# Sums of squares taken from transposed tiles, and stick-breaking products with v in groups of four key blocks

## The chip, the cores and the metric

One NeuronCore of one Trainium2 chip runs the whole program. The metric is device time in microseconds of one execution; the kernel before was timed in three runs. One further execution was recorded by the hardware profiler, and all stretches and durations below are of that one.

## The reference, cut to what matters

One layer (x is 1024 tokens by 1024 channels, fp32). A normalised x is multiplied by one wide matrix; its columns feed two token mixers and two merge gates.

```
h = RMSNorm(x);  proj = h @ w_in
A (8 heads of 64): z = q k^T / 8, causal; a = sigmoid(z) * prod over later keys of (1 - sigmoid(z)); o = a v
B (4 heads of 128): q, k, v = SiLU(conv4(.)); q, k each divided by sqrt(sum of squares over the 128 channels);
   chunked gated delta rule with k k^T, q k^T, a triangular solve and a scan over chunks; per-head RMSNorm
merged = sigmoid(gA) * (oA @ w_branch_sb) + sigmoid(gB) * (oB @ w_branch_gdn)
out = x + RMSNorm(merged @ w_out)
```

The change touches three places: the sums of squares of q and k in B, the product a v in A, and where some buffers of B and of the last stage are taken from.

## The kernel before, in words

Dense products run on TensorE (PE) as three fp32r matmuls of 512 columns per 128-row piece (high and low parts of both operands, `dense`, L222; `y`, L969). The transposes and the products `kk`, `kq`, `ss` and `av` have fp32 operands. PE takes its instructions in order. The program is written as generators, and `weave` interleaves dense work (`d_...` tiles) with the work that depends on other engines. A scheduler then fixes one order for each engine from the written order, priorities (`load_w` runs ahead) and the time at which it believes a buffer to be free.

Buffers: a slot pool `sp` with 23 slots of 4 KB a partition, a `small` pool in which tag `aT` has 4 buffers of 2 KB, and PSUM in two pools: 3 banks for dense outputs (`psd`) and 5 for all else (`psg`, `gps`). A bank is reused when its last reader is done.

Stages in order, with their time in the profile: the normalised input and first dense products; `g_mid(0)` (some 66 to 125 us), the solve and scan of heads 0 and 1, `g_mid(1)` (some 240 to 295 us), the scan of heads 2 and 3; the attention with its dense side work (500 to 817 us); `ya`, the product of A with its branch matrix (817 to 863 us); the last product `y` in two halves of 8 token tiles (to 953 us).

In `g_mid(b)` the convolved k and q of a head lie with channels on the partitions (`acc_k`, `acc_q`, 128x1024). `sumsq` squares such a tile on ScalarE (ACT, L375), sums over the partitions with eight matmuls against a column of ones (tile `ss_...`, L378) and copies 128x8 sums with VectorE (DVE, L379). `tokens` transposes k, eight 128x128 blocks into two banks (`t_k`, L386), and DVE copies them to `kn` (L387). The sums of k go into `br2`, which multiplies the products `kk` out of PSUM (L426), and those of q into `rqs`.

In the attention (`attention`, L781 onwards) a step is a pair of heads p and a query group g of two 128-query blocks. `sb_z` makes z on PE, two sigmoids on ACT (`kp` L800, `bt` L801), a scan on DVE (L803) and a product on GpSimd (POOL, L804). One step later `sb_av` transposes `bt` key block by key block (`aT`, L820, four 128x128 transposes, two for the last block), copies each out of PSUM (DVE L825 and L827, ACT L829), and multiplies with v (`av`, L834) after every two key blocks. At its end `sgT` is multiplied with `av` (L851).

In the last stage, `y` of a token tile is finished by: ACT squares and sums (L973, `yj` with tag `aT`), DVE multiplies with the norm weight (L978), a short chain for the root (L155 to L161), DVE adds the residual `xr` (L987, twice), and SyncE (SP) issues the output (L988) and the loads of `xr` (L982).

Of the kernel before, what the change touches and what calls it, by code (L numbers as in the profile page):

```python
# [7 lines left out]
F32 = mybir.dt.float32  # L8
# [12 lines left out]
CAP = 60.0  # L21
NSLOT = 23
AB = 4
RUN = 1.9
# [3 lines left out]
def tile_stickbreak_gdn_hybrid(  # L28
# [37 lines left out]
    def slot(name, dt=F32, shape=None):  # L66
        return sp.tile(shape or [P, T], dt, tag="s", name=name)

    def gps(name, shape=None):
        return psg.tile(shape or [P, 512], F32, tag="g", name=name)  # L70
# [301 lines left out]

    def sumsq(src, dst, h, name):
        sq = slot(f"sq_{name}")
        nc.scalar.activation(sq, src, AF.Square)  # L375
        ps = gps(f"ss_{name}")
        for c in range(NT):
            nc.tensor.matmul(ps[:, c:c + 1], lhsT=sq[:, c * P:(c + 1) * P], rhs=ones[:, 0:1], start=True, stop=True)  # L378
        nc.vector.tensor_copy(dst[:, h * NT:(h + 1) * NT], ps[:, :NT])  # L379

    def tokens(src, dst, name):
        for g in range(2):
            ps = gps(f"t_{name}_{g}")
            for j in range(4):
                c = g * 4 + j
                nc.tensor.transpose(ps[:, j * P:(j + 1) * P], src[:, c * P:(c + 1) * P], ident)  # L386
            nc.vector.tensor_copy(dst[:, g * 4:g * 4 + 4], ps.rearrange("p (c j) -> p c j", j=P))  # L387

# [106 lines left out]
    def g_lev(hs, last):  # L495
        lx, lxt = lane_out[hs[0] // 2]
        Xb, Xt = {}, {}
        for h in hs:
# [5 lines left out]
            for r in range(4):  # L504
# [3 lines left out]
                nc.sync.dma_start(Xb[h][rs, :, o:o + 32], lx[h % 2, r].rearrange("c i j -> i c j"))  # L508
        V1 = small.tile([P, 2, NT, 32], F32, tag="aT", name=f"V1_{hs[0]}", bufs=AB)
        ps = gps(f"V1p_{hs[0]}")  # L510
# [38 lines left out]
        for h in hs:  # L549
            V2[h] = small.tile([64, NT, 64], F32, tag="aT", name=f"V2_{h}", bufs=AB)  # L550
            src = pv[h][:64].rearrange("p (c j) -> p c j", j=64)
            if h % 2:
                nc.vector.tensor_scalar(V2[h], src, -1.0, None, op0=ALU.mult)
            else:
                nc.scalar.mul(V2[h], src, -1.0)
# [123 lines left out]
    def g_mid(b, prev):  # L679
        h0, h1 = 2 * b, 2 * b + 1  # L680
        bs = slice(b * 16, b * 16 + 16)
        drain(g_q(h0))
        for h in (h0, h1):
            kn[h] = slot(f"kn_{h}", shape=[P, NT, P])
            sumsq(kT[h], ssk, h, f"k{h}")
            tokens(kT[h], kn[h], f"k{h}")
        li = g_m(b)
        drain(g_q(h1))
        for h in prev:
            g_o(h)  # L690
        sumsq(qT[h0], ssq, h0, f"q{h0}")
        g_i(h0)
        drain(g_v(h0))
        drain(g_v(h1))
        sumsq(qT[h1], ssq, h1, f"q{h1}")
        rsqrt(rqs[:, bs], ssq[:, bs], 1.0, 16)
        nc.vector.tensor_scalar(rqs[:, bs], rqs[:, bs], float(P) ** -0.5, None, op0=ALU.mult)
        g_i(h1)
        last = lanes(b, li)
        ahead[0] = 600  # L700
        drain(fill(1))
        g_vt(h0)
        drain(fill(1))
        g_vt(h1)
        drain(fill(2), g_gate(h0), g_gate(h1))
        ahead[0] = 200
        return chain(g_lev((h0, h1), last), g_scan((h0, h1)))
# [72 lines left out]

    def sb_z(p, g):  # L781
        K, vn, gT, Q = sbd[p]
        QH, QL = Q[g // 2]
        for a in range(2):
            for j in range(2):
# [21 lines left out]
    def sb_av(p, g):  # L807
# [4 lines left out]

        def tr(c):
            j0 = 1 if c == cl else 0
            ps = gps(f"aT_{p}_{g}_{c}")
            for a in range(2):
                for j in range(j0, 2):
                    qb = 2 * g + j
                    off = c * P - (T - (qb + 1) * P)
                    nc.tensor.transpose(ps[:, (a * 2 + j) * P:(a * 2 + j + 1) * P], at[p, a, qb][:, off:off + P], ident)  # L820
            aT = small.tile([P, 4, P], F32, tag="aT", name="aT", bufs=AB)
            dst = aT.rearrange("p (a j) q -> p a j q", a=2)[:, :, j0:]
# [9 lines left out]
        def mm(c, j0, aT):  # L832
            for a in range(2):
                nc.tensor.matmul(av[a * 64:(a + 1) * 64, j0 * P:2 * P], lhsT=vn[:, c, a * 64:(a + 1) * 64],  # L834
                                 rhs=aT[:, a * 2 + j0:a * 2 + 2], start=(c == NT - 1), stop=(c == cl))

        q = []
        for c in range(NT - 1, cl - 1, -2):
            n = []
            for e in (c, c - 1):  # L840
                n.append(tr(e))
                yield 0.43
            for e in q:
                mm(*e)
            if q:
                yield 0.9
            q = n
        for e in q:
            mm(*e)
        yield 0.9  # L850
        nc.vector.tensor_tensor(gT[:, gq], gT[:, gq], av[:, :2 * P], op=ALU.mult)  # L851

    def attention():
        pend = []
        for p in range(NP):
            for g in range(NT // 2):
                yield from sb_z(p, g)
                pend.append((p, g))
                if len(pend) > 1:
                    yield from sb_av(*pend.pop(0))  # L860
            yield None
        yield from sb_av(*pend.pop(0))

# [90 lines left out]
    for n in range(2):  # L954
        ns = slice(n * HT, (n + 1) * HT)
        for t in range(NT):
# [8 lines left out]
            for c0, c1 in zip(cuts, cuts[1:]):  # L965
                ps = psd.tile([P, c1 - c0], F32, tag="d", name=f"y_{t}_{n}_{c0}")
                for k in range(NK):
                    for i, (a, b) in enumerate(((m_hi, wo[n, k][0]), (m_hi, wo[n, k][1]), (m_lo, wo[n, k][0]))):
                        nc.tensor.matmul(ps, lhsT=a[:, k, ts_], rhs=b[:, c0:c1], start=(k == 0 and i == 0),  # L969
                                         stop=(k == NK - 1 and i == 2))  # L970
                junk = small.tile([P, 4, P], F32, tag="aT", name="yj", bufs=AB)
                ss = small.tile([P, 1], F32, tag="ssy", name="ssy")
# [44 lines left out]
```

## Time and profile before

| what | before |
|---|---|
| median of 3 runs | 961.71 us (961.5 to 962.51) |
| the profiled execution | 960.5 us, of which the span of its instructions is 958.8 |
| busy share of the span | PE 98%, DVE 62%, ACT 39%, POOL 19% |
| granted TensorE clock | 0.999 of 2.4 GHz over the span |

Times in rows count from the start of the span. A row `start us, us, engine line op out<-in xcount` is one instruction or a run of equal ones. PE's matmuls are pipelined, and their ends are modelled: a row of a 128x512 product shows 0.39 us, and the next starts 0.227 us later. What a run of matmuls costs is read from its start to the start of the next row. Matmuls of fp32 operands stand as two records each.

### The profile page before, as it was taken

Reading aid. Unit: us, or ns where it says so; the run is one execution under the profiler, and the core shown is the slowest. Engines: PE = TensorE matmul, PEld = TensorE weight load, DVE = VectorE, ACT = ScalarE, POOL = GpSimd, SP = SyncE. Lnnn points to the kernel's source line nnn. Section 1 sums busy time; section 2 is a strip of 40 time slices with the busy share of each in tenths; the row PEclk is TensorE's granted clock in tenths of the full one; section 3 lists DMA queues with packets and bytes.
Section 4 is the critical chain, followed back from the end, with each engine's and each line's share of the span. In section 5 each row is a group of like instructions: output and inputs, shape, how many; then the busy total and the mean of one; then the engine's idle time right before and its main releaser. Section 6 shows DMA issues by size and latency. Waiting matters only on the chain.

```text
span 958.8 us, 13556 instructions
## 1 busy us (share of the span) xinstructions
PE 939.3 (98%) x5290; PEld 770.5 (80%) x5290; DVE 594.4 (62%) x1074; ACT 375.8 (39%) x741; POOL 185.1 (19%) x113
## 2 busy tenths in 40 slices
PE   8999999999999999999999999999999999999997
PEld 7978888788888887887877777877887777777886
DVE  5667796356899933656466734693675575573244
ACT  6664432135455112543244333462443453232221
POOL 1011210001113000000044212360533363341000
PEclk9999999999999999999999999999999999999999
DMA  7013324300221341005721121020011202772152
GB/s 254 14 45 95 98 72 132 67 24 23 67 77 56 110 115 40 12 23 184 235 77 45 29 60 44 23 67 23 23 44 44 78 34 64 248 266 80 58 193 102
DMA packets 88419, 80.12 MB, mean 84 GB/s; under 512 B 17098, under 2 KB 74531, under 8 KB 88355
## 3 DMA queue, kind: packets, MB, share of 16 engines
q1 hardware_dynamic: 86944, 79.20, 26.6%
q8 instruction: 41, 0.67, 0.3%
q10 hardware_dynamic: 1410, 0.07, 0.1%
q14 instruction: 24, 0.19, 0.1%
HBM read 60.88 MB, written 18.37 MB: 83 GB/s over the span
## 4 chain that ended last, share of the span: by engine, by line
PE 84%; DVE 7%; issue 3%; ACT 3%; DMA 2%; POOL 1%; DVEq 0%; ACTq 0%; POOLq 0%
PE d_mg L222 13%; PE y L969 8%; PE d_q L222 5%; PE d_sv L222 5%; PE d_gg L222 5%; PE d_v L222 5%; PE d_sk L222 5%; PE d_yb L222 4%; PE d_sq L222 4%; PE d_sgt L222 4%; PE av L834 4%; PE d_ya L222 3%; DVE kp L803 3%; PE aT L820 3%; PE d_k L222 2%
## 5 line engine op out<-in xcount | busy, mean ns | idle before, releaser
L804 POOL TENSOR_TENSOR bt<-bt,kp 128x127 f32<-128x127 f32 (+3 forms) x64 | 123.0, 1940 | 370.2 <-DVE kp L803 307.4
L803 DVE TENSOR_TENSOR_SCAN kp<-kp,mscan 128x128 f32<-128x128 f32 (+3 forms) x64 | 106.5, 1694 | 24.3 <-ACT kp L800 24.1
L222 PE MATMUL d_mg<-h_hi,whi_mg 128*128 128x512 f32 x256 | 101.5, 397 | 0.1
L222 PE MATMUL d_mg<-h_lo,whi_mg 128*128 128x512 f32 x256 | 100.1, 391 | 0.0
L222 PE MATMUL d_mg<-h_hi,wlo_mg 128*128 128x512 f32 x256 | 100.0, 391 | 0.0
L800 ACT ACTIVATE kp<-z 128x384 f32<-128x384 f32 (+4 forms) x96 | 49.6, 517 | 67.1 <-PE z L798 55.7
L222 PEld LDWEIGHTS d_mg<-h_hi,whi_mg 128*128 128x128 f32 x256 | 48.1, 188 | 10.9 <-issue 1.1
L222 PEld LDWEIGHTS d_mg<-h_hi,wlo_mg 128*128 128x128 f32 x256 | 48.1, 188 | 10.0
L222 PEld LDWEIGHTS d_mg<-h_lo,whi_mg 128*128 128x128 f32 x256 | 48.2, 188 | 9.3
L801 ACT ACTIVATE bt<-z 128x384 f32<-128x384 f32 (+4 forms) x96 | 50.1, 522 | 8.3 <-DMA mB_d<-mb 5.8
L969 PE MATMUL y<-wohi,m_lo 128*128 128x512 f32 (+1 forms) x136 | 51.4, 378 | 0.9 <-DVE m_lo L926 0.9
L969 PE MATMUL y<-wohi,m_hi 128*128 128x512 f32 (+1 forms) x136 | 51.4, 378 | 0.3 <-ACT m_hi L925 0.3
L969 PE MATMUL y<-wolo,m_hi 128*128 128x512 f32 (+1 forms) x136 | 51.3, 377 | 0.0
L834 PE MATMUL av<-aT,svn 128*64 128x256 f32 (+1 forms) x320 | 39.0, 369 | 3.5 <-DVE aT L825 1.2
L370 POOL TENSOR_TENSOR acc_k<-acc_k,pre_k 128x1024 f32<-128x1024 f32 x4 | 9.6, 2388 | 165.3 <-ACT pre_k L369 165.3
L820 PE MATMUL aT<-ident,bt 128*128 128x128 f32 x288 | 38.5, 276 | 2.2 <-DVE svn L772 1.8
L820 PEld LDWEIGHTS aT<-ident,bt 128*128 128x128 f32 x288 | 32.4, 140 | 9.8 <-issue 4.6
L834 PEld LDWEIGHTS av<-aT,svn 128*64 128x64 f32 x320 | 20.2, 136 | 20.5 <-issue 9.7
L89 ACT CAST whi_mg<-raw_mg 128x1024 fp32r<-128x1024 f32 x16 | 16.8, 1052 | 47.7 <-PE d_mg L222 25.5
L973 ACT ACTIVATE yj<-y 128x512 f32<-128x512 f32 (+1 forms) x17 | 9.7, 573 | 63.7 <-PE y L969 61.2
L941 POOL TENSOR_TENSOR sA<-sA,mBl 128x512 f32<-128x512 f32 x16 | 24.1, 1517 | 48.0 <-DVE sA L940 48.0
L90 DVE TENSOR_TENSOR wlo_mg<-raw_mg,whi_mg 128x1024 fp32r<-128x1024 f32 x16 | 23.3, 1454 | 13.6 <-ACT whi_mg L89 8.5
(381 smaller groups left out, 2448.0 us busy)
## 6 DMA issues: line engine op xcount, KB each, us to landing
raw_mg<-in_w_in_dram SPq DMA_DIRECT2D x16, 512.0 KB, 4.1
mg_d<-mg SPq DMA_DIRECT2D x16, 512.0 KB, 3.0
x<-in_x_dram SPq DMA_DIRECT2D x8, 512.0 KB, 6.9
mb<-mg_d SPq DMA_DIRECT2D x8, 512.0 KB, 5.8
mB_d<-mb SPq DMA_DIRECT2D x8, 512.0 KB, 3.7
sA<-mg_d SPq DMA_DIRECT2D x8, 512.0 KB, 6.8
mBl<-mB_d SPq DMA_DIRECT2D x8, 512.0 KB, 5.4
rawo<-in_w_out_dram SPq DMA_DIRECT2D x8, 512.0 KB, 4.9
```

The costliest lines, as they stand in the source:

```text
L89: nc.scalar.copy(hi[:, :nk], raw[:, :nk])
L90: nc.vector.tensor_sub(lo[:, :nk], raw[:, :nk], hi[:, :nk].bitcast(F32))
L222: nc.tensor.matmul(ps, lhsT=a[:, k], rhs=b[:, hs], start=(k == 0 and i == 0), stop=(k == nk - 1 and i == 2))
L800: nc.scalar.activation(kp[:, os_], ps[:, :pc], AF.Sigmoid, scale=-0.125)
L801: nc.scalar.activation(bt[:, os_], ps[:, :pc], AF.Sigmoid, scale=0.125)
L803: nc.vector.tensor_tensor_scan(kp[:, :n], kp[:, :n], mscan[:, :n], 1.0, op0=ALU.mult, op1=ALU.max)
L804: nc.gpsimd.tensor_tensor(bt[:, 1:n], bt[:, 1:n], kp[:, 0:n - 1], op=ALU.mult)
L820: nc.tensor.transpose(ps[:, (a * 2 + j) * P:(a * 2 + j + 1) * P], at[p, a, qb][:, off:off + P], ident)
L834: nc.tensor.matmul(av[a * 64:(a + 1) * 64, j0 * P:2 * P], lhsT=vn[:, c, a * 64:(a + 1) * 64], rhs=aT[:, a * 2 + j0:a * 2 + 2], start=(c == ...
L941: nc.gpsimd.tensor_tensor(ga[:, hs], ga[:, hs], mb[:, hs], op=ALU.add)
L969: nc.tensor.matmul(ps, lhsT=a[:, k, ts_], rhs=b[:, c0:c1], start=(k == 0 and i == 0), stop=(k == NK - 1 and i == 2))
L973: nc.scalar.activation(junk.rearrange("p a b -> p (a b)")[:, :c1 - c0], ps, AF.Square, accum_out=ss)
```

## The change

Two helpers, `sumsq` and `tokens`, become one. For k and for q it makes the eight transposes first; ACT then squares each transposed 128x128 block straight out of PSUM and adds along the row (`accum_out`, L384 of the new file), and only for k are the banks copied to `kn`. The matmuls with ones and the copies of their sums are gone. In the attention `sb_z` is called for each half (one head of the pair), `sb_av` multiplies after four key blocks, and its last run with the product on `gT` is handed back (`finish`, `late`) and placed between the halves of a later `sb_z`. `V1`, `V2`, `aT` (in pairs) and `yj` take slots of the slot pool, which has 25 now; tag `aT` is gone.

```diff
-NSLOT = 23
-AB = 4
+NSLOT = 25
...
-    def sumsq(src, dst, h, name):
-        sq = slot(f"sq_{name}")
-        nc.scalar.activation(sq, src, AF.Square)
-        ps = gps(f"ss_{name}")
-        for c in range(NT):
-            nc.tensor.matmul(ps[:, c:c + 1], lhsT=sq[:, c * P:(c + 1) * P], rhs=ones[:, 0:1], start=True, stop=True)
-        nc.vector.tensor_copy(dst[:, h * NT:(h + 1) * NT], ps[:, :NT])
-
-    def tokens(src, dst, name):
+    def sumsq(src, dst, h, name, keep=None):
+        pg = []
         for g in range(2):
             ps = gps(f"t_{name}_{g}")
             for j in range(4):
                 c = g * 4 + j
                 nc.tensor.transpose(ps[:, j * P:(j + 1) * P], src[:, c * P:(c + 1) * P], ident)
-            nc.vector.tensor_copy(dst[:, g * 4:g * 4 + 4], ps.rearrange("p (c j) -> p c j", j=P))
+            pg.append(ps)
+        for g, ps in enumerate(pg):
+            for j in range(4):
+                c = g * 4 + j
+                junk = small.tile([P, P], F32, tag="jk", name="jk")
+                nc.scalar.activation(junk, ps[:, j * P:(j + 1) * P], AF.Square,
+                                     accum_out=dst[:, h * NT + c:h * NT + c + 1])
+            if keep is not None:
+                nc.vector.tensor_copy(keep[:, g * 4:g * 4 + 4], ps.rearrange("p (c j) -> p c j", j=P))
...
+        def finish(q):
+            for e in q:
+                mm(*e)
+            yield 0.45 * len(q)
+            nc.vector.tensor_tensor(gT[:, gq], gT[:, gq], av[:, :2 * P], op=ALU.mult)
+
         q = []
-        for c in range(NT - 1, cl - 1, -2):
+        for c in range(NT - 1, cl - 1, -4):
             n = []
-            for e in (c, c - 1):
-                n.append(tr(e))
-                yield 0.43
+            for e in range(c, max(c - 4, cl - 1), -2):
+                pair = slot(f"aT_{p}_{g}_{e}", shape=[P, 2, 4, P])
+                for i in range(2):
+                    n.append(tr(e - i, pair[:, i]))
+                    yield 0.43
             for e in q:
                 mm(*e)
...
+        return finish(q)
...
-                yield from sb_z(p, g)
+                yield from sb_z(p, g, 0)
+                yield from late
+                late = iter(())
+                yield from sb_z(p, g, 1)
                 pend.append((p, g))
                 if len(pend) > 1:
-                    yield from sb_av(*pend.pop(0))
+                    late = yield from sb_av(*pend.pop(0))
...
-                junk = small.tile([P, 4, P], F32, tag="aT", name="yj", bufs=AB)
+                junk = slot(f"yj_{t}_{n}_{c0}", shape=[P, 4, P])
```

The order that the scheduler makes of it moves at three places. The first is PE in `g_mid(0)`, where `t_` are transposes, `ss_` the matmuls with ones, `kk` the products of k with itself and `d_q1` dense work. Before:

```order
L222 MATMUL d_q1_0_966<-h_hi_189,wlo_q1_962 128x512
L378 MATMUL ss_k0_823<-ones_136,sq_k0_821 128x1 x8
L386 MATMUL t_k0_0_833<-ident_111,acc_k0_740 128x128 x4
L386 MATMUL t_k0_1_839<-ident_111,acc_k0_740 128x128 x4
L222 MATMUL d_q1_0_966<-h_hi_189,whi_q1_961 128x512
...
L378 MATMUL ss_k1_848<-ones_136,sq_k1_846 128x1 x8
L386 MATMUL t_k1_0_858<-ident_111,acc_k1_747 128x128 x4
L386 MATMUL t_k1_1_864<-ident_111,acc_k1_747 128x128 x4
L421 MATMUL kk_0_0_885<-acc_k0_740 128x128 x4
```

and now:

```order
L390 MATMUL rw_730<-ident_111,GG_715 32x128
L378 MATMUL t_k0_0_821<-ident_111,acc_k0_740 128x128 x4
L378 MATMUL t_k0_1_826<-ident_111,acc_k0_740 128x128 x4
L378 MATMUL t_k1_0_850<-ident_111,acc_k1_747 128x128 x4
L378 MATMUL t_k1_1_855<-ident_111,acc_k1_747 128x128 x4
L421 MATMUL kk_0_0_893<-acc_k0_740 128x128 x4
...
L378 MATMUL t_q0_0_1033<-ident_111,acc_q0_813 128x128 x4
L221 MATMUL d_v0_0_1089<-h_hi_189,whi_v0_1084 128x512
L221 MATMUL d_v0_0_1089<-h_lo_190,whi_v0_1084 128x512
L378 MATMUL t_q0_1_1038<-ident_111,acc_q0_813 128x128 x4
```

Both heads' transposes of k now stand in one row ahead of the first `kk`; twelve dense matmuls lie between `kk_0_0` and the other three `kk`, and the transposes of q0 stand behind all four.

The second place is PE in the attention of the first pair of heads, third query group. Before:

```order
L820 MATMUL aT_0_2_4_4932<-ident_111,bt_0_1_5_4640 128x128
L834 MATMUL av_0_2_4874<-aT_4880,svn_0_4000 64x256 x2
L834 MATMUL av_0_2_4874<-aT_4887,svn_0_4000 64x256 x2
L820 MATMUL aT_0_2_3_4943<-ident_111,bt_0_0_4_4598 128x128
...
L834 MATMUL av_0_2_4874<-aT_4894,svn_0_4000 64x256 x2
L834 MATMUL av_0_2_4874<-aT_4937,svn_0_4000 64x256 x2
L834 MATMUL av_0_2_4874<-aT_4948,svn_0_4000 64x256 x2
L834 MATMUL av_0_2_4874<-aT_4953,svn_0_4000 64x128 x2
```

and now, where `z_1_..` belongs to the next pair of heads:

```order
L819 MATMUL aT_0_2_2_5004<-ident_111,bt_0_1_5_4741 128x128
L832 MATMUL av_0_2_4943<-aT_0_2_7_4944,svn_0_4072 64x256 x4
L832 MATMUL av_0_2_4943<-aT_0_2_5_4984,svn_0_4072 64x256 x4
L221 MATMUL d_sq1_0_4974<-h_hi_189,whi_sq1_4970 128x512
...
L797 MATMUL z_1_0_1_0_5147<-KA_1_4581,QL_1_0_5032 128x256
L832 MATMUL av_0_2_4943<-aT_0_2_3_4997,svn_0_4072 64x256 x2
L832 MATMUL av_0_2_4943<-aT_0_2_3_4997,svn_0_4072 64x128 x2
L796 MATMUL z_1_1_0_0_5161<-KB_1_4582,QH_1_0_5031 128x128
```

The runs of `av` are fewer and longer, and the last of a group stands between two `z`.

The third place is SP in the last stage (`xr` the residual's loads, `out` the output's stores). Before:

```order
L982 DMA xr_0_7914<-in_x_dram 128x1024
L982 DMA xr_1_7958<-in_x_dram 128x1024
L982 DMA xr_2_8002<-in_x_dram 128x1024
L982 DMA xr_3_8046<-in_x_dram 128x1024
L982 DMA xr_4_8090<-in_x_dram 128x1024
L982 DMA xr_5_8134<-in_x_dram 128x1024
L988 DMA out_0_dram<-y_0_7611 128x512 x2
L982 DMA xr_6_8178<-in_x_dram 128x1024
```

and now:

```order
L990 DMA xr_0_7946<-in_x_dram 128x1024
L996 DMA out_0_dram<-y_0_7643 128x512 x2
L990 DMA xr_1_7990<-in_x_dram 128x1024
L996 DMA out_0_dram<-y_1_7675 128x512 x2
L990 DMA xr_2_8034<-in_x_dram 128x1024
L996 DMA out_0_dram<-y_2_7713 128x512 x2
L990 DMA xr_3_8078<-in_x_dram 128x1024
```

Each load but the first stands behind the two stores of the tile before it, to the end of the program.

## Rows read from the trace of the kernel before

**Rows 1.** The page: busy time and share of each engine; granted clock.

```profile
PE 939.3 (98%) x5290; PEld 770.5 (80%) x5290; DVE 594.4 (62%) x1074; ACT 375.8 (39%) x741; POOL 185.1 (19%) x113
PEclk9999999999999999999999999999999999999999
```

**Rows 2.** Waits of PE, attention's five: releaser: us in total, times, longest.

```profile
PE aT L820 <- DVE svn L772: 1.8, 1, 1.8
PE av L834 <- DVE aT L825: 1.2, 2, 0.6
PE av L834 <- DVE aT L827: 1.1, 1, 1.1
PE av L834 <- ACT aT L829: 1.0, 2, 0.6
PE aT L820 <- ACT bt L801: 0.4, 1, 0.4
```

**Rows 3.** Timeline of PE, 69 to 85 us: `ss`, transposes and `kk`.

```profile
69.66 1.84 PE L378 MATMUL ss_k<-ones,sq_k 128*128 128x1 f32 x16
71.36 1.07 PE L386 MATMUL t_k<-ident,acc_k 128*128 128x128 f32 x8
72.19 0.48 PE L222 MATMUL d_q<-h_hi,whi_q 128*128 128x512 f32 x1
...
80.37 1.07 PE L386 MATMUL t_k<-ident,acc_k 128*128 128x128 f32 x8
81.28 3.74 PE L421 MATMUL kk<-acc_k 128*128 128x128 f32 x32
```

**Rows 4.** PE's groups by shape: two records a matmul with ones, 8 runs.

```profile
L378 PE MATMUL ss_q<-ones,sq_q 128*128 128x1 f32 x64 | 7.6, 248 | 0.2 <-ACT sq_q L375 0.2
L378 PE MATMUL ss_k<-ones,sq_k 128*128 128x1 f32 x64 | 7.4, 245 | 0.0
```

**Rows 5.** ACT, timeline 414 to 415 us: squares of 128x128 with a sum.

```profile
414.12 0.39 ACT L640 ACTIVATE jk<-vb,rqs 128x128 f32<-128x128 f32 x1
414.42 0.19 ACT L640 ACTIVATION_READ_ACCUMULATOR jk<-vb,rqs 128x1 f32 x1
414.51 0.39 ACT L640 ACTIVATE jk<-vb,rqs 128x128 f32<-128x128 f32 x1
```

**Rows 6.** DVE, timeline 81 to 93 us: copies of k, decay tiles, first products on `kk`.

```profile
81.12 1.22 DVE L387 COPY kn<-t_k 128x512 f32<-128x512 f32 x2
...
84.60 2.18 DVE L402 SCALAR_TENSOR_TENSOR D-1.0_0_874<-D-1.0_0_874,GG,capm 128x128 f32<-128x128 f32 x8
86.70 2.19 DVE L402 SCALAR_TENSOR_TENSOR D-1.0_1_907<-D-1.0_1_907,GG,capm 128x128 f32<-128x128 f32 x8
...
89.31 1.12 DVE L426 SCALAR_TENSOR_TENSOR D-1.0_0_874<-kk,br,D-1.0_0_874 128x128 f32<-128x128 f32 x4
```

**Rows 7.** Busy time by stretch: PE, PEld, DVE, ACT, POOL, clock, DMA share, GB/s.

```profile
66.00:95.00 29.00, 28.89 (x171) 25.10 (x170) 22.00 (x71) 14.36 (x18) 2.71 (x2) 1.00 0.26 75
236.00:290.00 54.00, 54.00 (x307) 46.59 (x306) 47.31 (x112) 25.92 (x47) 7.19 (x3) 1.00 0.23 64
```

**Rows 8.** Timeline of PE in the attention: runs of 8 and of 16 records.

```profile
657.51 0.39 PE L222 MATMUL d_sk<-h_hi,wlo_sk 128*128 128x512 f32 x1
657.83 1.08 PE L834 MATMUL av<-aT,svn 128*64 128x256 f32 x8
658.85 0.87 PE L820 MATMUL aT<-ident,bt 128*128 128x128 f32 x6
659.65 1.08 PE L834 MATMUL av<-aT,svn 128*64 128x256 f32 x8
660.66 0.50 PE L222 MATMUL d_sk<-h_hi,whi_sk 128*128 128x512 f32 x1
661.00 0.39 PE L222 MATMUL d_sk<-h_lo,whi_sk 128*128 128x512 f32 x1
...
697.80 1.73 PE L834 MATMUL av<-aT,svn 128*64 128x256 f32 x16
699.47 0.47 PE L797 MATMUL z<-KA,QH 128*128 128x448 f32 x1
```

**Rows 9.** DVE in the last stage: adding the residual, tiles 0, 1 and 7.

```profile
917.27 1.42 DVE L987 SCALAR_TENSOR_TENSOR y<-y,ry,xr 128x512 f32<-128x512 f32 x2
...
921.82 1.41 DVE L987 SCALAR_TENSOR_TENSOR y<-y,ry,xr 128x512 f32<-128x512 f32 x2
...
954.34 1.41 DVE L987 SCALAR_TENSOR_TENSOR y<-y,ry,xr 128x512 f32<-128x512 f32 x2
```

**Rows 10.** SP's queue from 918 us.

```profile
918.05 1.01 SPq L988 DMA_DIRECT2D out_dram<-y  x2
919.11 2.25 SPq L982 DMA_DIRECT2D xr<-in_x_dram  x2
```

**Rows 11.** Issue to landing: the load at 919.11; one at 921; all eight (last line).

```profile
xr<-in_x_dram SPq DMA_DIRECT2D x1, 512.0 KB, 3.8
...
xr<-in_x_dram SPq DMA_DIRECT2D x1, 512.0 KB, 5.1
...
DMA to landing us min/median/max: 3.6/4.8/7.2
```

## What the change should do to the time

> **What bounds the kernel.** I read the page first. PE is busy for 98% of the span at full clock, and no other engine passes 62% [rows 1]. PE takes its instructions in order, so the time is the length of PE's queue, and a gain is either a record less on PE or a wait less in front of one. The waits of PE come next. Of the attention's, those of `av` for a copy just before it make 1.2 + 1.1 + 1.0 = 3.3 us, and two others make 1.8 and 0.4 [rows 2], 5.5 in all. Matmul ends are modelled, so I took each price from the start of a run to the start of the next. Last I read the end of the program, where PE is done and a chain of DVE, SP and a load decides [rows 9 to 11].
>
> **Part 1, the matmuls with ones.** A run of eight (16 records) lasts from 69.66 to 71.36, 1.70 us [rows 3]; there are 128 records, so eight runs [rows 4]. Removed: 8 x 1.70 = 13.6. Added: transposes of q for four heads. Eight transposes take 0.83 (71.36 to 72.19) or 0.91 (80.37 to 81.28) [rows 3]: 4 x 0.87 = 3.5. PE's queue is shorter by **10.1 us**. The transposes of k stay.
>
> The squares move from eight of 128x1024 to 64 of 128x128 on ACT, each with its sum. Such a pair of instructions exists and follows itself every 0.39 us (414.12 to 414.51) [rows 5]: 3.1 us a head. ACT has the time in the mean, 14.4 of 29 us busy in the first of the two stages and 25.9 of 54 in the second [rows 7]; if that cover goes, the price is a wait for a PSUM bank. And some of that wait I expect, since the transposed banks of k are now read by four squares and only then copied by DVE.
>
> In `g_mid(0)` both heads' squares take 16 x 0.39 = 6.2 us and can start when PE has the transposes, about where `ss_k` started, 69.7. So they end near 75.9. In the kernel before DVE needs from its copy of `kn` at 81.12 to the end of the first products on `kk` (89.31 + 1.12 = 90.4), 9.3 us, decay tiles included [rows 6]. The same 9.3 us behind 75.9 give 85.2 for the first bank of `kk`. PE did `kk` from 81.28 for about 3.5 us (3.74 less the modelled end) [rows 3], to 84.8; without two `ss_k` that is 81.4. Eight dense matmuls (1.8), `t_q0_0` (0.45) and two dense ones (0.45) follow, so PE comes at 84.1 to `t_q0_1`, which takes the bank of the first `kk`. It waits 1.0 to 1.4 us; I take 1.3. `kq_0_1` then needs a bank that four squares (1.6 us) still read, of which dense work covers about half: 0.7. Together **+2.0**, between 0 (DVE reaches `kk` sooner) and 5.1 (all that this stage gains, 2 x 1.70 for k and 2 x 0.83 for q).
>
> In `g_mid(1)` DVE is busy 47.3 of 54 us [rows 7]. PE comes earlier by its own gain, DVE doesn't, and the outputs of the earlier heads need banks that DVE frees after its products on `kk`. I put the wait at **+2.0**, between 0 and 5.1 for the same reason. Part 1 sums to -10.1 + 2.0 + 2.0 = -6.1.
>
> The Trainium skill (ScalarE: Activation LUTs, What ACT_TABLE_LOAD costs) gives 186 ns plus 0.833 ns an element for such an ACTIVATE and 93 ns of overlap, so by an estimate from that page 0.20 us a square. No row here shows that, since the square with its sum repeats at 0.39; by the page the squares would end 3 us sooner, both waits of `g_mid(0)` would be gone, and the sum would be 2.0 us lower.
>
> **Part 2, runs of `av`.** Going into a run from a dense matmul costs 0.32 instead of 0.227 (657.51 to 657.83), and the first dense matmul after one 0.34 (660.66 to 661.00). Two runs of 8 records take 1.02 and 1.01 us, one of 16 takes 1.67 (697.80 to 699.47) [rows 8]. So two runs joined save 2.03 - 1.67 = 0.36 and with both edges 0.36 + 0.09 + 0.11 = 0.56; where transposes follow, nearly nothing. I count 33 runs before and 23 after, 10 less, and take the middle, 0.32: **-3.2**, between 0 and -5.6. There are 10 more runs of `z`, for which I see no edge between `z` and dense rows, and put 0.
>
> **Part 3, waits in the attention.** `av` now follows its copies by two more key blocks or, in the late run, by a whole `z`. So the 3.3 us should go. The 1.8 us, a bank that DVE frees behind scans (`svn`), and the 0.4 us for `bt` don't hang on `av`; moved by a little, I let 0.7 of 2.2 go. **-4.0**, between 0 and -5.5 [rows 2]. Four key blocks need four banks of five for their transposes while `av` holds the fifth; I count nothing for it, since the blocks before are copied by then. If that fails, each wait is of the 0.6 us size in rows 2. The pairs of `aT` hold slots that `kp` and `bt` also use; two more slots replace what tag `aT` had, and ACT, which would wait, is 39% busy [rows 1]. At the end of the attention the last multiplications can't be covered by a `z`: **+0.3**, half of such a wait.
>
> **Part 4, the end.** `yj` in slots changes when slots for `xr` come free, and SP now loads `xr` of a tile only behind the stores of the tile before it. DVE's addition (L987) of tile 0 starts at 917.27; the stores go at 918.05, the next load at 919.11, 1.84 us behind the addition [rows 9, 10]. That load took 3.8 us behind two stores, just the new situation [rows 11]. With 0.1 us from landing to start, an estimate, the period is 1.84 + 3.8 + 0.1 = 5.74 us. The additions were 954.34 - 917.27 = 37.1 us apart over seven tiles, 5.30 each [rows 9]. New: 7 x 5.74 = 40.2, so **+3.1**. Bounds: 0 at a landing under 3.36, +1.7 at the shortest seen, 3.6, and +12.2 at the 5.1 of the load at 921 [rows 11]. I take 3.8 because it is the one row with the same neighbours.
>
> The Trainium skill (DMA: Bandwidth & Descriptors, Anatomy of one DMA) has about 2.0 us plus bytes at 436 GB/s, an estimate of 3.2 us for 512 KB. By it the period would be 5.1, PE would set the pace and the sum would be 3.1 us lower; all eight loads here took 3.6 or more, which speaks against it.
>
> **Sum.** -6.1 - 3.2 - 4.0 + 0.3 + 3.1 = -9.9. The profiled execution took 960.5, so 950.6 for one like it. The median of the three runs is 961.71, 1.2 above it: **951.8 us**.
>
> **Rivals.**
> All covered: no new bank waits, all 5.5 us of waits gone, loads no later than PE. -10.1 - 3.2 - 5.5 = -18.8, so 942.9. For it: ACT half idle. Against: DVE in the second stage, and 3.6 as the shortest load. 0.14.
>
> Part 1 given back: DVE, not PE, sets both stages, and PE waits at banks for all that it saved (0 for part 1). -3.2 - 4.0 + 0.3 + 3.1 = -3.8, so 957.9. For it: 47.3 of 54 us of DVE. Against: it still loses eight small copies, and the first stage has 7 of 29 us free. 0.16.
>
> The change to `av` does nothing: the waits come back at other banks, and joined runs are those where transposes follow. -6.1 + 0.3 + 3.1 = -2.7, so 959.0. 0.07.
>
> Slower, by the end's chain alone: loads wait behind stores and land late. The rest is worth -13.0, so it decides at (37.1 + 13.0) / 7 = 7.16 us a tile, a landing of 5.2. At 5.1 it is -0.8, no change; at the longest landing seen, 7.2, the period is 9.14, the end 64.0 - 37.1 = 26.9 later, and the time 975.6. For it: half of the eight loads took 4.8 or more. Against: those were issued several at a time, and here one stands alone. 0.06 for slower, 0.04 for no change.
>
> **How the numbers follow.** The forecast has 0.53. Measurements of this kernel tell some 0.2%, 1.9 us, from no change. The forecast, full cover and the two partial cases are faster, 0.90, less some 0.03 for partial cases that end within 1.9 us: 0.87. Within it 0.04 + 0.02, slower 0.06 + 0.01. The range leaves out half of the full cover at its lower end, and the chain and a little of the partial cases at its upper: 943.5 to 959.5.
>
> **What would show it.** In the new trace: no rows with ones, 64 squares of 0.39 us; PE waiting 1 to 2 us for DVE near 84 us and once in the second stage; some 23 runs of `av`, none waiting on `aT`; L987 about 5.7 us apart, waiting for a load, not for ACT. Wrong if PE waits at banks for more than 5 us in the two stages, if `kp` starts to wait for slots and PE for `kp`'s banks, or if the additions are 5.3 or over 6 us apart.

## The result, and the profile after

| what | before | after |
|---|---|---|
| median of four runs each | 962.11 us (961.5 to 965.39) | 952.41 us (951.52 to 953.58) |
| ratio | | 0.990 [0.988, 0.9921] |
| the profiled execution, its span | 960.5, 958.8 | 953.58, 951.8 |
| granted TensorE clock | 0.999 | 0.996 |

The total came out as forecast (951.8), but not by the forecast's terms. The profiled execution of the new kernel is the slowest of its four, that of the kernel before lies below all its four runs; so the two spans differ by 7.0 us where the medians differ by 9.7. The table splits those 7.0 us at the first and last matmuls of the stages, as the trace has them. The last two columns belong to experiments that are told below.

| stretch, us | before | after | difference | e6_both | e9_later |
|---|---|---|---|---|---|
| start to the first product on `vn` (with `g_mid(0)`) | 126.95 | 122.53 | -4.4 | 122.5 | 121.3 |
| to the first `d_sk` (with `g_mid(1)`) | 234.2 | 232.2 | -2.0 | 234.0 | 232.0 |
| to the first `aT` | 127.5 | 127.2 | -0.3 | 127.3 | 127.2 |
| attention, to the first `d_ya` | 329.5 | 319.7 | -9.8 | 319.7 | 319.7 |
| `ya`, to the first `y` | 45.0 | 49.8 | **+4.8** | 43.8 | 43.8 |
| `y`, to its last matmul | 89.05 | 88.35 | -0.7 | 87.2 | 87.2 |
| last matmul to the end | 6.6 | 12.0 | **+5.4** | 6.6 | 6.6 |

So the parts that were meant to gain gained 16.5 us, and 10.2 us were lost in two stages behind them. First the page of the new kernel, to be held against [rows 1]: PE has 96 records less and is a little less busy, 97% of a shorter span.

```profile
PE 924.6 (97%) x5194; PEld 760.5 (80%) x5194; DVE 591.0 (62%) x1066; ACT 384.9 (40%) x861; POOL 166.4 (17%) x113
PEclk9999999999999999999999999999999999999998
```

The waits of PE in the new kernel (releaser, us in total, times, longest):

```profile
PE d_ya L221 <- DVE wlo_wbs L89: 3.8, 2, 1.9
PE oT L656 <- DVE gg L657: 1.8, 1, 1.8
PE t_q L378 <- DVE D-1.0_0_882 L426: 1.2, 1, 1.2
...
PE d_ya L221 <- DVE sA L948: 1.1, 1, 1.1
PE av L832 <- DVE aT L825: 1.1, 1, 1.1
PE d_mg L221 <- ACT mg L676: 1.0, 1, 1.0
...
PE y L977 <- ACT m_hi L933: 0.5, 1, 0.5
```

Of the attention's five waits [rows 2] one is left, 1.1 us. New are `t_q` in `g_mid(0)`, `oT` and, just behind, `d_mg` in `g_mid(1)`, and 4.9 us for `d_ya`, which waited 0.8 before.

**The squares.** In ACT's timeline they follow one another every 0.25 us, not every 0.39 as those that I took the price from [rows 5]:

```profile
70.36 0.29 ACT L384 ACTIVATE jk<-t_k 128x128 f32<-128x128 f32 x1
70.52 0.23 ACT L384 ACTIVATION_READ_ACCUMULATOR jk<-t_k 128x1 f32 x1
70.61 0.30 ACT L384 ACTIVATE jk<-t_k 128x128 f32<-128x128 f32 x1
```

Sixteen of them are through between 69.23 and 73.6. DVE is not ready for `kk` then. It copies the four banks of `kn` up to 75.1, and one instruction of 128x16 (L149), which takes 0.17 us at 79.10, takes 2.26 us at 76.18. It ends at 78.44, just behind an addition of POOL that ends at 78.41:

```profile
76.18 2.26 DVE L149 TENSOR_SCALAR rst<-rst 128x16 f32<-128x16 f32 x1
```

```profile
76.03 2.38 POOL L369 TENSOR_TENSOR acc_q<-acc_q,pre_q 128x1024 f32<-128x1024 f32 x1 [9.86 <-ACT pre_q L368]
```

DVE reads the first bank of `kk` only from 84.11, and PE's `t_q` starts in that bank 1.18 us later:

```profile
84.11 2.15 DVE L426 SCALAR_TENSOR_TENSOR D-1.0_0_882<-kk,br,D-1.0_0_882 128x128 f32<-128x128 f32 x8
```

```profile
85.29 0.66 PE L378 MATMUL t_q<-ident,acc_q 128*128 128x128 f32 x4 [1.17 <-DVE D-1.0_0_882 L426]
```

**`ya`.** The diff has no line here, but the scheduler orders the whole program, and DVE now does the split of one half (`m_lo`) ahead of the multiplication `sA` of the next. DVE, POOL and ACT of the new kernel, in that stage:

```profile
824.35 0.69 DVE L934 TENSOR_TENSOR m_lo<-sA,m_hi 128x512 fp32r<-128x512 f32 x1 [1.84 <-ACT m_hi L933]
824.96 0.68 DVE L948 TENSOR_TENSOR sA<-sA,d_ya 128x512 f32<-128x512 f32 x1
825.77 1.29 POOL L949 TENSOR_TENSOR sA<-sA,mBl 128x512 f32<-128x512 f32 x1 [2.11 <-DVE sA L948]
827.10 0.62 ACT L933 CAST m_hi<-sA 128x512 fp32r<-128x512 f32 x1 [2.78 <-POOL sA L949]
827.75 0.69 DVE L934 TENSOR_TENSOR m_lo<-sA,m_hi 128x512 fp32r<-128x512 f32 x1 [2.11 <-ACT m_hi L933]
828.36 0.68 DVE L948 TENSOR_TENSOR sA<-sA,d_ya 128x512 f32<-128x512 f32 x1
```

Read down: `sA` at 824.96 releases POOL, POOL releases ACT, ACT releases `m_lo` at 827.75, and only behind that stands the next `sA`, at 828.36. It is a loop over four instructions in which each waits for the one before, 828.36 - 824.96 = 3.4 us a half. A half in which DVE also splits new weights took longer, 832.59 - 828.36 = 4.2. PE needs 12 matmuls of 0.227 us, 2.72 us, for a half. Late as DVE is, its split of the next weights (`wlo_wbs`) comes late too, and PE waits 1.9 us twice for that (the last section shows these two splits). In the kernel before two `sA` stand together, and the loop is cut:

```profile
831.15 0.68 DVE L940 TENSOR_TENSOR sA<-sA,d_ya 128x512 f32<-128x512 f32 x1
832.08 0.69 DVE L940 TENSOR_TENSOR sA<-sA,d_ya 128x512 f32<-128x512 f32 x1 [0.25 <-PE d_ya L222]
```

**The end.** DVE's additions (L995 now) of tiles 0, 1, 5 and 7; then SP's queue; then issue to landing of the eight loads:

```profile
904.86 1.42 DVE L995 SCALAR_TENSOR_TENSOR y<-y,ry,xr 128x512 f32<-128x512 f32 x2
910.95 1.42 DVE L995 SCALAR_TENSOR_TENSOR y<-y,ry,xr 128x512 f32<-128x512 f32 x2 [1.57 <-DMA xr<-in_x_dram]
...
935.01 1.42 DVE L995 SCALAR_TENSOR_TENSOR y<-y,ry,xr 128x512 f32<-128x512 f32 x2 [3.88 <-DMA xr<-in_x_dram]
...
947.42 1.42 DVE L995 SCALAR_TENSOR_TENSOR y<-y,ry,xr 128x512 f32<-128x512 f32 x2 [3.07 <-DMA xr<-in_x_dram]
```

```profile
905.64 1.01 SPq L996 DMA_DIRECT2D out_dram<-y  x2
906.74 0.40 SPq L990 DMA_DIRECT2D xr<-in_x_dram  x1
```

```profile
DMA to landing us min/median/max: 3.5/3.9/4.8
```

From the second on, every addition waits for its load, and the load goes out behind the addition before it: 1.82 to 1.91 us behind in six periods, 3.05 in the one in which SP's two stores (at 935.79) took 2.18 us instead of about 1.0. The additions are (947.42 - 904.86) / 7 = 6.08 us apart, against 5.30 before [rows 9].

### The profile page after: what moved, and what is told of

Same layout as the page of the kernel before. It is cut to its first block, busy times and chain, and to the rows that moved or that the text cites. A ratio compares the mean times of both kernels' runs of the same rounds, so it can differ in the third digit from the quotient of the medians.

```text
span 951.8 us, 13464 instructions
## 1 busy us (share of the span) xinstructions
PE 924.6 (97%) x5194; PEld 760.5 (80%) x5194; DVE 591.0 (62%) x1066; ACT 384.9 (40%) x861; POOL 166.4 (17%) x113
## 4 chain that ended last, share of the span: by engine, by line
PE 81%; DVE 9%; DMA 4%; ACT 2%; issue 2%; POOL 2%; SPq 0%; DVEq 0%; POOLq 0%; ACTq 0%
PE d_mg L221 17%; PE y L977 6%; PE d_sk L221 5%; PE d_sv L221 5%; PE d_gg L221 5%; PE d_sgt L221 5%; PE d_yb L221 4%; PE d_sq L221 4%; PE d_v L221 4%; PE av L832 4%; PE aT L819 3%; PE d_k L221 2%; PE d_k L211 2%; DMA xr<-in_x_dram 2%; PE z L796 2%
## 5 line engine op out<-in xcount | busy, mean ns | idle before, releaser
L803 POOL TENSOR_TENSOR bt<-bt,kp 128x127 f32<-128x127 f32 (+3 forms) x64 | 102.6, 1613 | 380.6 <-DMA mb<-mg_d 155.4
L802 DVE TENSOR_TENSOR_SCAN kp<-kp,mscan 128x128 f32<-128x128 f32 (+3 forms) x64 | 103.8, 1640 | 26.3 <-ACT kp L799 26.0
L221 PEld LDWEIGHTS d_mg<-h_hi,whi_mg 128*128 128x128 f32 x256 | 48.1, 188 | 12.5 <-issue 1.7
L221 PEld LDWEIGHTS d_mg<-h_hi,wlo_mg 128*128 128x128 f32 x256 | 48.1, 188 | 10.2
L832 PE MATMUL av<-aT,svn 128*64 128x256 f32 (+1 forms) x320 | 36.8, 366 | 1.1 <-DVE aT L825 1.1
L819 PE MATMUL aT<-ident,bt 128*128 128x128 f32 x288 | 36.5, 273 | 0.0
L949 POOL TENSOR_TENSOR sA<-sA,mBl 128x512 f32<-128x512 f32 x16 | 26.2, 1643 | 51.6 <-DVE sA L948 49.5
L676 ACT ACTIVATE mg<-d_mg 128x512 f32<-128x512 f32 x32 | 19.1, 602 | 31.0 <-PE d_mg L221 28.3
```

The source lines that it names most:

```text
L221: nc.tensor.matmul(ps, lhsT=a[:, k], rhs=b[:, hs], start=(k == 0 and i == 0), stop=(k == nk - 1 and i == 2))
L676: nc.scalar.activation(gt[:, hs], ps, AF.Sigmoid)
L802: nc.vector.tensor_tensor_scan(kp[:, :n], kp[:, :n], mscan[:, :n], 1.0, op0=ALU.mult, op1=ALU.max)
L803: nc.gpsimd.tensor_tensor(bt[:, 1:n], bt[:, 1:n], kp[:, 0:n - 1], op=ALU.mult)
L949: nc.gpsimd.tensor_tensor(ga[:, hs], ga[:, hs], mb[:, hs], op=ALU.add)
```

## The experiments

Times are medians; ratios are to the kernel before on the same chip. A second measurement of the changed kernel itself gave 953.65 us, 0.9916 [0.9903, 0.993], with the same stages within 0.6 us.

**e1_yj: the changed kernel with `yj` in a buffer of its own** (of bf16; the squares took 0.60 us as before), so that no slot of `xr` is tied to it.

```diff
-                junk = slot(f"yj_{t}_{n}_{c0}", shape=[P, 4, P])
+                junk = small.tile([P, 4, P], BF16, tag="yj", name="yj", bufs=1)
```

> The changed kernel with one edit: the scratch output of the squares of y (yj) is a bf16 tile of the small pool and takes no slot. By that SP's order in the last stage is the one of the kernel before: six loads of the residual at once, then stores. Theory (loads behind stores set the end): the seven additions L995 of the changed kernel lie 6.08 us apart where PE's tiles lie 5.44 apart; with the loads ahead the end follows PE again and the span loses the 5.4 us that it lost between PE's last product and the end: about 947 us against 952.4. Rival (the additions are late for another cause, the chain of ACT and DVE ahead of them): additions still about 6 us apart, time within 1 us of 952.4.

Measured: 948.54 us, 0.9872 [0.9858, 0.9885]. SP issues all eight loads by 906.7, no addition waits for one, and the last stretch is back at 6.6 us. The additions:

```profile
904.38 1.41 DVE L995 SCALAR_TENSOR_TENSOR y<-y,ry,xr 128x512 f32<-128x512 f32 x2
...
941.40 0.75 DVE L995 SCALAR_TENSOR_TENSOR y<-y,ry,xr 128x512 f32<-128x512 f32 x1
```

They are 37.0 us apart over seven tiles, 5.29 each, as before the change. The spans of the two profiled executions differ by 6.0 us, the ratios by 0.3 to 0.4%, some 3 to 4 us. The place is plain from the trace: the +5.4 us of the end hang on the slots of `yj`. The loads themselves took longer here (3.8 to 7.1 us, median 5.5, issued in a bunch) and cost nothing.

**e2_sums and e3_att: each part alone on the kernel before.** e2_sums has only the new `sumsq` with its `accum_out`; e3_att only the attention, the slots, `yj` among them.

```diff
+    def sumsq(src, dst, h, name, keep=None):
...
+                nc.scalar.activation(junk, ps[:, j * P:(j + 1) * P], AF.Square,
+                                     accum_out=dst[:, h * NT + c:h * NT + c + 1])
...
-            sumsq(kT[h], ssk, h, f"k{h}")
-            tokens(kT[h], kn[h], f"k{h}")
+            sumsq(kT[h], ssk, h, f"k{h}", kn[h])
```

```diff
-NSLOT = 23
+NSLOT = 25
...
-        for c in range(NT - 1, cl - 1, -2):
+        for c in range(NT - 1, cl - 1, -4):
...
-                yield from sb_z(p, g)
+                yield from sb_z(p, g, 0)
+                yield from late
+                late = iter(())
+                yield from sb_z(p, g, 1)
```

> The kernel before with the sums-of-squares part alone; attention, buffers and pools as before. Theory: PE gains 13.6 - 3.5 = 10.1 us of queue and loses some 4 at PSUM banks in the two g_mid stages; in the trace of the full change the two stages gave 4.3 and 2.0 to 2.3. So 962.1 - 6.3 = 955.8, a wait of t_q for the products on kk (about 1.2) and one of oT (about 1.8) in the waits of PE, and the last stages as in the kernel before. Rival (the stage is DVE's, the gain is given back): 961 to 962. Rival (all covered): 952.

> The changed kernel with the sums of squares of the kernel before: attention part and slot buffers alone. Theory (parts add): attention -9.8 to -10.1, the stage ya +4.1 to +4.8, the end +5.4, in sum about 0 to -1: 961 to 962. Rival (the losses of ya and of the end hang on PE coming early by the sums of squares, so they are not of this part): 952 to 956.

Measured: e2_sums 957.83 us, 0.9971 [0.9959, 0.9982]; e3_att 960.01 us, 0.9986 [0.9977, 0.9995]. e3_att held: attention -9.8, `ya` +4.9, `y` -0.7, end +4.6. The attention's part alone gains 9.8 us and gives nearly all of it back behind the attention, by `ya` and the end. Which of its lines makes the new order in `ya` is open.

e2_sums gained about 3 us where 6.3 were expected. At the first `aT` it stands at -5.1, with a longer wait behind `g_mid(1)` than the whole change has:

```profile
PE d_mg L222 <- ACT mg L677: 2.3, 1, 2.3
PE oT L657 <- DVE gg L658: 2.1, 1, 2.1
```

And it lost another 1.6 us in an attention that it doesn't touch. The first table is e2_sums by stretches of 2 us (PE, PEld, DVE, ACT, POOL busy, granted clock, DMA share, GB/s), the second the kernel before at the same place of the program:

```profile
522.00:524.00 2.00, 0.49 (x4) 0.42 (x4) 2.00 (x5) 0.90 (x2) 2.00 (x1) 1.00 0.00 0
524.00:526.00 2.00, 2.00 (x9) 1.71 (x8) 2.00 (x3) 0.59 (x1) 2.00 (x2) 0.55 0.00 0
526.00:528.00 2.00, 2.00 (x7) 1.57 (x6) 2.00 (x1) 0.00 (x0) 0.46 (x1) 0.59 0.00 0
528.00:530.00 2.00, 2.00 (x10) 1.61 (x9) 1.87 (x3) 1.55 (x2) 1.22 (x1) 1.00 0.00 0
```

```profile
526.00:528.00 2.00, 0.77 (x6) 0.44 (x4) 2.00 (x3) 1.98 (x4) 2.00 (x1) 1.00 0.00 0
528.00:530.00 2.00, 1.42 (x10) 1.20 (x11) 2.00 (x4) 0.59 (x1) 2.00 (x2) 1.00 0.00 0
```

Both wait 1.8 us for `svn`. In one execution the granted clock fell to the lower of its two levels, 1.2 GHz, behind the wait (0.55 and 0.59 of 2.4 GHz in the mean of two stretches), in the other it did not. The two parts, -0.29% and -0.14%, do not add up to the whole, -0.84 to -1.0%. In the profiles the spans of the parts fell by 3.0 and 1.4 us, that of the whole by 7.0. The longer `oT` and `d_mg` waits of e2_sums make 1.6 us of this and the clock another 1.6; a longer `y` in e2_sums (0.5) and a shorter end in e3_att (0.9) nearly cancel. The medians differ by more, 4 to 5.5 us; what is beyond the 2.6 of the profiles is not explained.

**e4_first: the weights' split in `ya` ahead of the other splits** (the splits of `m` and of `w_out` wait for it, and the load of the next weights is drawn ahead by one block; of this edit only a part is shown). It asks whether PE's `d_ya` waits hang on `wlo_wbs`, the releaser that the list names.

```diff
...
-                split_m(*pend.pop(0))
+                with tc.issue_after(wsp[0].ins), tc.issue_after(wsp[1].ins):
+                    split_m(*pend.pop(0))
...
```

> The changed kernel with one edit of order in the stage ya: the split of the next weights (whi_wbs, wlo_wbs) stands ahead of the casts of w_out (wohi, wolo), which the changed kernel has in front of it. Theory (a cast of 1.05 us on ACT and one of 1.22 on DVE stand in front of the split for which PE waits twice for 2.1 us): both waits go or fall under 0.5 us, ya is 3 to 4 us shorter, time 948.5 to 949.5. Rival (the split is late because POOL and DVE slow each other and m_hi waits for POOL): the waits stay over 1.5 us each, time within 1 us of 952.4.

Measured: 953.89 us, 0.9929 [0.9915, 0.9943], no gain over the changed kernel. `ya` takes 49.6 us, and the waits have only changed their names:

```profile
PE d_ya L223 <- DVE sA L953: 2.6, 3, 0.9
...
PE y L984 <- ACT m_hi L935: 1.2, 1, 1.2
```

That theory fell. From 822.86 on the splits of the weights take 0.7 us each and PE waits for none of them, but the loop is still there (`sA` at 825.99 and 829.38, 3.4 us apart) and `ya` is as long. So DVE, held up in the loop, was late for everything.

**e5_lag: the split of a finished half only behind the next half's `sA`.** It cuts the loop of four and touches nothing else.

```diff
-            nc.vector.tensor_tensor(ga[:, hs], ga[:, hs], ps, op=ALU.mult)
+            sa = nc.vector.tensor_tensor(ga[:, hs], ga[:, hs], ps, op=ALU.mult)
...
-                split_m(*pend.pop(0))
+                with tc.issue_after(sa.ins):
+                    split_m(*pend.pop(0))
```

> The changed kernel with one edit of order in ya: the split of a finished half (m_hi on ACT, m_lo on DVE) stands behind DVE's product sA of the next half. In the changed kernel m_lo of a half stands ahead of sA of the next, so sA, POOL's addition, m_hi and m_lo run one after another, 3.4 us a half (L948 at 821.23, 824.96, 828.36) where PE needs 2.72. Theory (this loop is what ya lost): ya from 49.8 to 44.5 to 45.5 us, PE's waits for wlo_wbs gone, time 4 to 5 us under that of the changed kernel on the same chip. Rival (DVE has too much to do in ya, or POOL and DVE slow each other): ya stays above 48 us as in e4_first.

Measured: 945.81 us, 0.9831 [0.9818, 0.9845]. That is 7.8 us under the changed kernel measured beside it, more than the 4 to 5 expected. `ya` takes 43.8 us, 6.0 less than in the changed kernel and 1.2 less than before, `y` 1.1 less and the end 1.0 to 1.4 less, and no wait for `d_ya` or `y` is left in the list. DVE of e5_lag now has `sA` before `m_lo`:

```profile
822.61 0.68 DVE L948 TENSOR_TENSOR sA<-sA,d_ya 128x512 f32<-128x512 f32 x1
823.20 0.69 DVE L934 TENSOR_TENSOR m_lo<-sA,m_hi 128x512 fp32r<-128x512 f32 x1
824.48 0.69 DVE L948 TENSOR_TENSOR sA<-sA,d_ya 128x512 f32<-128x512 f32 x1 [0.59 <-PE d_ya L221]
```

Here `sA` waits for PE, as it should. DVE's order, with the loop in it, is shown to be the cause of the loss in `ya`. The same edit also moved the splits of weights out of POOL's way (last section), so how much of the 6.0 us is the loop alone is not shown.

**e6_both: e1_yj and e5_lag together** (both diffs above).

> The changed kernel with both repairs, the scratch output of y's squares outside the slots (e1_yj) and the lag in ya (e5_lag). If the two losses are apart, their gains add: 3 to 5.5 and 4 to 5 us under the changed kernel on the same chip, 941.5 to 944.5 us. If a shorter ya only makes the last stage wait, it ends within 1 us of the better of the two.

Measured: 942.35 us, 0.9795 [0.9781, 0.9808], and in a second measurement 942.41, 0.9799 [0.9786, 0.9813]. Both fixes hold beside each other: 3.5 us below e5_lag, with additions 5.29 apart.

**e7_nolate: groups of four, but the last run at once**, without the late part.

```diff
-                yield from late
-                late = iter(())
...
-                    late = yield from sb_av(*pend.pop(0))
+                    yield from (yield from sb_av(*pend.pop(0)))
```

> The changed kernel without the late part: the last run of a query group and its product follow at once, groups of four key blocks stay. Theory (the 5.4 us of waits in the attention went because the last run no longer stands right behind its transposes, the other 4.4 by fewer runs): the waits of av on aT come back, one a group, 16 groups at 0.3 to 0.6: the attention 4 to 6 us longer than in the changed kernel, time 955 to 957. Rival (groups of four alone take the waits away): within 1 us of the changed kernel.

Measured: 969.24 us, 1.0073 [1.0059, 1.0086], slower than the kernel before. The direction was expected, the size was not. Its attention takes 336.1 us, 16.4 more than the changed kernel's and 6.6 more than that of the kernel before:

```profile
PE av L832 <- DVE aT L825: 6.2, 7, 1.3
...
PE av L832 <- DVE aT L823: 2.9, 5, 1.0
...
PE aT L819 <- DVE svn L771: 1.8, 1, 1.8
PE aT L819 <- DVE aT L825: 1.6, 2, 0.8
```

These waits make 12.5 us against 1.1, and two more runs and one drop of the clock behind `svn` some 2 us more. The other 3 us or so are not assigned. Groups of four are worth having only with the late part: with them a run stands right behind the copies of its own last blocks.

**e8_two: the late part kept, groups of two.**

```diff
-        for c in range(NT - 1, cl - 1, -4):
+        for c in range(NT - 1, cl - 1, -2):
...
-            for e in range(c, max(c - 4, cl - 1), -2):
+            for e in range(c, max(c - 2, cl - 1), -2):
```

> The changed kernel with multiplications after two key blocks instead of four, the late part and everything else kept: 41 runs of av in PE's order where the changed kernel has 23 and the kernel before 33. Theory (a run of av costs about 0.3 to 0.45 us of changing over, and the late part by itself takes the waits away): the attention 18 x 0.3 to 18 x 0.45 = 5.5 to 8 us longer than in the changed kernel, no wait of av over 1 us, time 958.5 to 961. Rival (runs cost nothing where transposes follow, the whole gain is the late part): within 1.5 us of the changed kernel.

Measured: 958.58 us, 0.9973 [0.9962, 0.9983]. There are 41 runs of `av` in its trace against 23, and its attention is 7.1 us longer at full clock. The waits for `aT` (1.6 + 0.6 instead of 1.1) make 1.1 of that; (7.1 - 1.1) / 18 = 0.33 us a run, beside the 0.32 that the prediction took.

**e9_later: e6_both with `oT`, the transposes of q and `kq` one dense tile later** (the dense tile `d_v` of the next head is drawn ahead of them).

```diff
+        drain(g_v(h0))
...
-        drain(g_v(h0))
```

> The kernel with both repairs and one move in g_mid: the outputs of the earlier heads (oT), the transposes of q and kq stand one dense tile (two halves, 10.9 us) later. Theory (part 1 lost 1.3 us in the first g_mid and 2.2 in the second because PE asks for banks that DVE has not yet freed, and nothing else waits for those transposes): both waits go, 2.5 to 3.5 us less than the kernel with both repairs, about 939. Rival (DVE is behind in the whole second stage, so the wait turns up at the next bank, kq or the gates): within 1 us of it.

Measured: 940.52 us, 0.9782 [0.9768, 0.9796], the fastest of all: 2.2% under the kernel before, 1.9 us under e6_both. Held in part. The 1.2 us of `t_q` in `g_mid(0)` and the 2.0 of `oT` in `g_mid(1)` are gone, but in `g_mid(1)` and behind it smaller waits stand in their place, 2.3 us in all:

```profile
PE d_mg L221 <- ACT mg L676: 0.7, 1, 0.7
PE kq L472 <- DVE D1.0_2_2788 L475: 0.7, 1, 0.7
PE kq L472 <- DVE gg L657: 0.6, 1, 0.6
...
PE t_q L378 <- DVE gg L657: 0.3, 1, 0.3
```

DVE is busy in 56.1 of the 60 us from 240 to 300, and there a later bank mostly moved the wait. The first stage is 1.2 us shorter than in e6_both, the second 2.0, but most of these 2.0 are a drop of the clock that e6_both had there (last section): against the changed kernel, which had none, the second stage gained 0.2.

## Why the prediction was right, and where it was not

- **Part 1, -6.1: right**, -6.7 in the trace from the start to the first `aT`. In `g_mid(0)` the wait of `t_q` was 1.2 (I took 1.3) and the first bank of `kk` came free at about 85.2 as in the sum, but by luck. The squares were through at 73.6, not 75.9, and DVE began its copies at 72.60. From there to 85.2 it took 12.6 us where I had 9.3: the copies of both heads now stand in one row (2.46 us instead of 1.22), and the instruction that ended with POOL's addition took 2.1 longer. By these rows the bank would have been free 2.1 us sooner without that, before PE came for it at 84.1; no run shows it. The 0.7 for `kq` did not occur, since the squares repeat at 0.25. In `g_mid(1)` `oT` waited 1.8 (I took 2.0), and the `d_mg` wait of 1.0 was not foreseen.
- **The square's price, 0.39, was wrong.** The row was a square of `vb`, a buffer in SBUF, and with a scale for each partition (`rqs` stands in it as an input); these read PSUM and have no scale, and repeat at 0.25. Other rows of the traces point to the scale: an ACTIVATE of 128x128 from PSUM with a factor for each partition (`qs`, L587) takes 0.37 us in the mean, one without (`bt`, L801 before) 0.29, the square of `vb` 0.39. The Trainium skill (ScalarE: Activation LUTs, What ACT_TABLE_LOAD costs) led to an estimate of 0.20, nearer to the trace than my row. But "both waits of `g_mid(0)` would be gone" did not follow: the wait of `t_q` hangs on DVE, not on ACT.
- **Runs of `av`, 0.32 each: right**, 0.33 by e8_two; 10 runs fewer are 3.3 us. **Waits, -4.0:** the five listed waits fell from 5.5 to 1.1, -4.4. Together -7.7 of the -9.8 measured. Where the other 2.1 us lie, the rows show when each is counted from its start to the next start, idle time apart. Idle time fell by 4.7 us. Of as many instructions as before, dense ones took 2.9 less, `aT` 1.8 less, `av` 1.5 less and `z` 1.1 more. Dense work now stands in 43 runs instead of 52, `aT` in 30 instead of 35, `z` in 40 instead of 30. That fits a price for each change between kinds of work, as in the sum, but the sum had it for `av` alone and put `z` at nothing. The +0.3 for the end of the attention was not seen on its own.
- **The end, +3.1: the right mechanism, too small.** It measured +5.4. The period was 6.08 and not 5.74. In the mean of the seven periods the load was issued 2.04 us behind the addition (1.84 in the sum, from one row) and the next addition started 4.04 behind the issue (3.9 in the sum, again from one row; landings reached 4.8). Seven periods more of 0.34 are 2.4, which is the difference. The Trainium skill (DMA: Bandwidth & Descriptors, Anatomy of one DMA) gives its fit for DMAs that GpSimd issues; by it I had 3.2 us, and nothing would be lost. These loads are issued by SP, and none landed under 3.3 in any run here, so the measurement decides against it.
- **`ya`: the term that was missing.** The sum has nothing for a stage that the diff doesn't touch, and the trace has +4.8, shown by e5_lag to come from a new order of DVE's instructions there, and by e3_att to come with the attention's part of the change. The order of the changed program was to be had before the run; I read it at the places that the diff names and not here.
- **The sum.** Against the forecast the terms are off by -0.6 (part 1), -2.9 (attention), +4.8 (`ya`), -0.7 (`y`) and +2.3 (the end), +2.9 together: -7.0 in the trace where -9.9 stood. The median still came within 1 us of 951.8, because the profiled execution of the new kernel is its slowest, 1.2 above its median, and that of the kernel before 1.6 below the median of its four runs. So the total was met by luck as much as by the sum: errors cancelled. Of the rivals, full cover described the attention best (the waits gone but for one), and the slower one named the right chain at the end, whose period of 6.08 stayed under its limit of 7.16.

## What to carry to other kernels

After a change to a kernel whose order a scheduler makes, compare the order of every stage, not only of those in the diff, and look for loops over several engines in which one engine's instruction for the last piece stands ahead of that for the next. A scratch buffer put into a shared pool ties the reuse of that pool to its reader: give the output of an instruction that nobody reads its own buffer. Here a long run of matmuls paid only with its operands ready well ahead: groups of four without the late part (969.24 us) were slower than groups of two (958.58 with the late part, 962.11 in the kernel before).

## What the runs showed of the hardware that I had not expected

- **A wait of PE can cost more than its length.** Behind a wait of some 2 us the granted clock fell to the lower of its two levels, 1.2 GHz, in some executions and not in others. In e6_both behind the 2.04 us for `oT`, by stretches:

```profile
258.00:260.00 2.00, 0.40 (x4) 0.40 (x5) 2.00 (x9) 1.10 (x2) 0.00 (x0) 1.00 0.00 0
260.00:262.00 2.00, 2.00 (x12) 1.71 (x11) 2.00 (x9) 1.38 (x2) 0.00 (x0) 0.76 0.00 0
262.00:264.00 2.00, 2.00 (x9) 1.60 (x8) 2.00 (x7) 0.00 (x0) 0.00 (x0) 0.50 0.32 50
```

  Its matmuls then start 0.43 us apart instead of 0.227 (261.85, 262.28, 262.70). From the first `vn` to the first `d_sk` e6_both took 234.0 us and the changed kernel, with a wait of 1.8 and no drop, 232.2. With a wait of 2.0 at the same place, the second measurement of the changed kernel had no drop either. So part of the spread between executions may come from this, and a gain of 1 or 2 us needs more than one of them.
- **DVE and POOL took turns** in `ya`. A split of 128x512 (`wlo_wbs`) takes DVE 0.69 us (821.83), an addition takes POOL 1.29 (825.77). Where they meet, in the new kernel:

```profile
828.96 1.22 DVE L925 TENSOR_TENSOR wolo<-rawo,wohi 128x1024 fp32r<-128x1024 f32 x1
830.09 1.75 DVE L89 TENSOR_TENSOR wlo_wbs<-raw_wbs,whi_wbs 128x512 fp32r<-128x512 f32 x1
```

```profile
829.12 2.18 POOL L949 TENSOR_TENSOR sA<-sA,mBl 128x512 f32<-128x512 f32 x1 [2.05 <-DVE sA L948]
```

  `wolo` came first and takes its usual 1.22. POOL, begun at 829.12, ends at 831.30, 1.1 us after `wolo`; `wlo_wbs`, begun at 830.09, ends at 831.84, 0.5 us after POOL. Each ends about as if it had begun when the other was done, and so does L149 in `g_mid(0)` above. The two splits that PE waited for are the two that met POOL so (830.09 and 837.71, 1.75 us each); in e5_lag, where the order differs, the splits from 821.39 on take 0.69. It was read from these rows, and no run was made for it alone. The Trainium skill (SBUF — State Buffer, SBUF: two separate sides) states such an exclusive lock for a DVE instruction with two SBUF inputs against a GpSimd one that reads SBUF; the rows in `ya` agree with it.
